# A hybrid decoder layer on one core: cache pages read with four keys per partition, each V tile by one indirect transfer

## The chip, the core and the metric

The kernel runs on one core of a Trainium2 chip. The metric is the device time of one launch in microseconds (us); a run is the median of several executions. Engines are named as in the profile: PE (TensorE, matrix products), DVE (VectorE), ACT (ScalarE), POOL (GpSimd) and SP (SyncE, which here only issues transfers). DMA engines move data between HBM and the on-chip memory SBUF; products land in PSUM.

## What is computed

One decoder layer over 256 prompt tokens and 64 sample tokens (8 sequences of 8 new tokens, each with 2048 cached keys in 16 pages of 128 keys, found through a page table). The layer is a feed-forward block, a mixer of two head groups, and a second feed-forward block. The part that matters here is the sample side of head group A: an indexer picks 256 keys for each query, and attention runs over these. The kernel does it as dense attention over all 2112 keys with a mask, since a key that is not picked gets a very large negative logit:

```python
def sparse_attend(q, qi, wi, pos_q, ki_all, gather_kv, top, rel_bias):
    ...
    _, idx = lax.top_k(score, top)
    valid = idx <= pos_q[None, :, None]
    k_sel, v_sel = gather_kv(idx)
    qg = q.reshape(b, nq, N_KV_HEADS, GQA_GROUP, HEAD_DIM)
    logits = jnp.einsum('bqkgd,bqskd->bqkgs', qg, k_sel).astype(jnp.float32) * HEAD_DIM ** -0.5
    bias = rel_bias[t5_bucket(jnp.maximum(pos_q[None, :, None] - idx, 0))]
    ...
    p = jax.nn.softmax(logits, axis=-1).astype(v_sel.dtype)
    out = jnp.einsum('bqkgs,bqskd->bqkgd', p, v_sel)
```

A softmax over keys and the sum over keys after it don't depend on the order of the keys, as long as logits, mask, bias and values use one order. A page of the K or V cache is 128 keys by 2 heads by 128 numbers in fp32: 1 KB per key, 128 KB per page, contiguous in HBM.

## The kernel before

The program runs in stages: the first feed-forward block (`run_ffn`, L249), the projections of the indexer and its scores (L545 to L717), the threshold search of the top-k (L741 to L770), the projections of q, k and v, then the **sample attention** (L1062 to L1172) together with prompt attention heads (L829) and the last projections (`proj_xbc`, `conv_out`, `proj_z`, L1176 to L1180), then the state-space heads (`ssd_group`, L903) with the output projection `w_out` (L1230), and the second feed-forward block.

A projection streams its weights in chunks of 512 KB (`raw`, three buffers). ACT rounds a chunk to `hi` (L162), DVE makes the remainder `lo` (L163), and PE does three products per tile (L173 to L175). In the sample attention stage the chunks of `w_in` are issued from ACT's queue (`wq[0] = S`, L1174).

The sample attention takes the 8 sequences in 4 pairs `i`, and the 2048 keys of each in 4 blocks `kb` of 4 pages. The loop at L1155 works on the logits of pair `i` and on the outputs of pair `i - 1` in the same turn:

- `load_k` (L1068): per sequence one tile `kn` (512 KB, two buffers in all) from 4 pages, each its own transfer on SP's queue, whose page number SP reads from the page table (`pages`, L508). PE turns each 128 x 128 piece over (L1077, 8 per tile), ACT and DVE copy the result from PSUM (`kt`, L1079).
- `logits_part` (L1083): one mask product (L1085) and four products of the queries with the keys (L1086) into one PSUM tile, copied to `pr` (L1088). After the last block come the new tokens' own keys (L1094), the bias of near keys (L1097) and the softmax (L1098 to L1102).
- `sample_pT` (L1105): 17 transposes of the probabilities.
- `load_v` (L1121) and `out_part` (L1135): two tiles `vn` of 4 pages (512 KB each, four buffers in all), 16 small products (L1136). Of each pair of tiles the first comes through 4 indirect transfers on POOL's queue (L1131), with row numbers from the table `pti`; the second, and both for the last pair, through 4 page transfers on SP's queue (L1129).

The order of the work on PE, ACT, DVE and POOL is not the order of the text: a scheduler in the framework places the instructions when the program is built, by its own costs. Only SP's order in this stage is that of the text (`manual_schedule`, L1064). So a change of the transfers can move other work, projections above all. On the chip every engine then runs its list strictly in order.

Of the kernel before, what the change touches and what calls it, by code (L numbers as in the profile page):

```python
# [10 lines left out]
F32 = mybir.dt.float32  # L11
# [3 lines left out]
I32 = mybir.dt.int32  # L15
AF = mybir.ActivationFunctionType
ALU = mybir.AluOpType
# [4 lines left out]
P = 128  # L22
# [3 lines left out]
NB = 8  # L26
# [7 lines left out]
PAST, PG = 2048, 128  # L34
NPG = PAST // PG
# [10 lines left out]
SK = PAST + TS  # L46
# [3 lines left out]
C_TS, C_TST, C_OH, C_DT, C_TT, C_PI = 512, 576, 640, 1024, 1040, 1048  # L50
# [38 lines left out]
def tile_kernel(tc, I, O, ffn=True):  # L89
    nc = tc.nc  # L90
    V, S, G, TE, SY = nc.vector, nc.scalar, nc.gpsimd, nc.tensor, nc.sync
# [12 lines left out]
    def nm(s):  # L104
        uid[0] += 1
        return f"{s}_{uid[0]}"
# [4 lines left out]
    def pm():  # L111
        return psM.tile([P, 512], F32, tag="m", name=nm("pm"))

    def pa_():
        return psA.tile([P, 512], F32, tag="a", name=nm("pa"))
# [4 lines left out]
    def block(mms, inputs):  # L120

        for m in inputs:
            tc.add_manual_dep(mms[0].ins, m.ins.name, SYNC, reason="block inputs")
        for a, b in zip(mms, mms[1:]):
            tc.add_manual_dep(b.ins, a.ins.name, NOSYNC, reason="block order")
# [3 lines left out]
    def pf():  # L129
        flip[0] += 1  # L130
        return (pw, pm, pa_, pm, pa_, pw, pm, pa_)[(flip[0] - 1) % 8]()

    cst = base.tile([P, C_N], F32, tag="cst", name="cst")
# [10 lines left out]
    def pe_t(out, in_):  # L144
        n = in_.shape[0]
        TE.transpose(out, in_, cst[:n, C_ID:C_ID + n])  # L146
# [181 lines left out]
    per = tc.alloc_tile_pool(name="per", bufs=1)  # L328
# [4 lines left out]
    mkS = per.tile([P, HK], BF, tag="mkS", name="mkS")  # L333
    mkP = per.tile([P, 2, TP], BF, tag="mkP", name="mkP")
    ptb = per.tile([1, NB * NPG], I32, tag="ptb", name="ptb")
    ptc = per.tile([NB * NPG, 1], I32, tag="ptc", name="ptc")
    pti = per.tile([P, NB * NPG], I32, tag="pti", name="pti")
    Rep = per.tile([P, 2, 4, P], BF, tag="Rep", name="Rep")
    saO = per.tile([P, NH, TS], F32, tag="saO", name="saO")
    bS = per.tile([P, 192], F32, tag="bS", name="bS")  # L340
# [88 lines left out]
    pt_flat = I["page_table"].rearrange("b g -> (b g)")  # L429
    SY.dma_start(ptc, pt_flat[:, None])  # L430
    SY.dma_start(ptb, pt_flat[None, :])
    SY.dma_start(pti, pt_flat[None, :].to_broadcast([P, NB * NPG]))
    V.tensor_scalar(pti, pti, float(PG), cst[:, C_PI:C_PI + 1], op0=ALU.mult, op1=ALU.add)
    G.memset(Rep, 0.0)
    for i in range(4):
        sel = cst[:TS, C_ID + 16 * i:C_ID + 16 * i + 16].rearrange("p (b t) -> p b t", b=2)[:, :, None, :].to_broadcast([TS, 2, NH, NS])
# [1 line left out]
            V.tensor_scalar(Rep[TS * half:TS * half + TS, half, i, :].rearrange("p (b h t) -> p b h t", b=2, h=NH), sel, NEG, None, op0=ALU.mult)  # L438

    pre = tc.alloc_tile_pool(name="pre", bufs=1, side="right")  # L440
    csT = per.tile([P, 12, 29], F32, tag="csT", name="csT")
    pc = pm()
    for q in range(3):
# [64 lines left out]
    def pages(pool, b, g0, n):  # L508
        _, vs = nc.values_load_multi_w_load_instructions(ptb[0:1, b * NPG + g0:b * NPG + g0 + n], engines=[SPE], min_val=0, max_val=NPOOL - 1,
                                                         skip_runtime_bounds_check_because="page_table holds page numbers of the pool, as the reference's indexing has it")  # L510
        return [pool[0, ds(v, 1)].rearrange("o p v d -> (o p) (v d)") for v in vs]

    def project(c0, evac):
        ps = [pw(), pw()]
# [45 lines left out]
    for tt in range(3):  # L560
        n = P if tt < 2 else TS
# [19 lines left out]
    def sm(tag):  # L581
        return per.tile([P, 3, SH], F32, tag=tag, name=nm(tag))

    v, e, s_, s2, dt, dA = sm("v"), sm("e"), sm("s_"), sm("s2"), sm("dt"), sm("dA")
# [92 lines left out]
    for u in range(NU):  # L677
# [22 lines left out]
        for par in range(2):  # L700
            src = ps[TS * par:TS * par + TS, :256].rearrange("p (q k g) -> p g k q", q=2, k=8)
# [127 lines left out]
    for h in range(NH):  # L829
        hk = pa.tile([P, 384], F32, tag="hk", name=nm("hk"), bufs=1)  # L830
        src = r_scr[h:h + 1, 0:512]
        SY.dma_start(hk, bass.AP(tensor=src.tensor, offset=src.offset, ap=[[1, P], [1, 384]]))
        kv = h // GQ
        p, pt, po = pm(), pm(), pm()
# [3 lines left out]
        for qt in range(2):  # L838
            nk = P * (qt + 1)
            lg = p[:, lo_[qt]:lo_[qt] + nk]  # L840
# [3 lines left out]
        for qt in range(2):  # L844
            nk = P * (qt + 1)
            lg = p[:, lo_[qt]:lo_[qt] + nk]
# [212 lines left out]
        project(Z0 + j * P, evac)  # L1059


    cv = I["cache_v"][0].rearrange("n k v d -> (n k) (v d)")  # L1062
    order = ExitStack()
    order.enter_context(tc.manual_schedule(engines={SPE}))  # L1064
    def qs(i, q):
        return qS[:, 2 * i + q // 2, 4 * (q % 2):4 * (q % 2) + 4, :].rearrange("p g t -> p (g t)")

    def load_k(i, kb):  # L1068
        kts, made = [], []
        for bb in range(2):  # L1070
            kn = sa.tile([P, 4, 256], F32, tag="kn", name=nm("kn"), bufs=2)
            for g, src in enumerate(pages(I["cache_k"], 2 * i + bb, 4 * kb, 4)):
                SY.dma_start(kn[:, g, :], src)
            for kv in range(2):
                pt = pa_()
                for g in range(4):
                    pe_t(pt[:, g * P:(g + 1) * P], kn[:, g, kv * P:(kv + 1) * P])  # L1077
                kt = sa.tile([P, 512], F32, tag="kt", name=nm("kt"), bufs=5)
                made.append(V.tensor_copy(kt, pt) if kv else S.copy(kt, pt))  # L1079
                kts.append(kt)  # L1080
        return kts, made

    def logits_part(i, kb, pr_, mx, kts, made):  # L1083
        lg = pa_()
        TE.matmul(lg, Rep[:, kb // 2, i, :], mkS[:, 512 * (kb % 2):512 * (kb % 2) + 512], start=True, stop=False)  # L1085
        mms = [TE.matmul(lg[32 * q:32 * q + 32], qs(i, q), kts[q], start=False, stop=True) for q in range(4)]  # L1086
        block(mms, made)
        S.copy(pr_[:, 512 * kb:512 * kb + 512], lg)  # L1088
        if kb < 3:
            V.tensor_reduce(mx[:, kb:kb + 1], pr_[:, 512 * kb:512 * kb + 512], axis=AX.X, op=ALU.max)  # L1090
            return mms
        lg = pa_()
        TE.matmul(lg[:, :TS], Rep[:, 1, i, :], mkS[:, PAST // 2:HK], start=True, stop=False)
        last = [TE.matmul(lg[32 * q:32 * q + 32, :TS], qs(i, q), kT[:, q % 2, TP:T], start=False, stop=True) for q in range(4)]  # L1094
        block(mms[-1:] + last, [])
        S.copy(pr_[:, PAST:SK], lg[:, :TS])
        V.tensor_add(pr_[:, PAST - P:SK], pr_[:, PAST - P:SK], bS)  # L1097
        V.tensor_reduce(mx[:, 3:4], pr_[:, 3 * 512:SK], axis=AX.X, op=ALU.max)  # L1098
        V.tensor_reduce(mx[:, 5:6], mx[:, 0:4], axis=AX.X, op=ALU.max, negate=True)
        S.activation(pr_, pr_, AF.Exp, bias=mx[:, 5:6], accum_out=mx[:, 6:7])  # L1100
        V.reciprocal(mx[:, 6:7], mx[:, 6:7])
        V.tensor_scalar(pr_, pr_, mx[:, 6:7], None, op0=ALU.mult)  # L1102
        return mms + last
# [17 lines left out]
    def load_v(i, kb):  # L1121
        vns, made = [], []
        for bb in range(2):
            vn = sa.tile([P, 4, 256], F32, tag="vn", name=nm("vn"), bufs=4)
            on_sp = pages(I["cache_v"], 2 * i + bb, 4 * kb, 4) if bb or i == 3 else None
            for g in range(4):
                pg_i = (2 * i + bb) * NPG + 4 * kb + g
                if on_sp is not None:
                    made.append(SY.dma_start(vn[:, g, :], on_sp[g]))  # L1129
                else:  # L1130
                    made.append(G.indirect_dma_start(out=vn[:, g, :], out_offset=None, in_=cv, in_offset=bass.IndirectOffsetOnAxis(ap=pti[:, pg_i:pg_i + 1], axis=0)))  # L1131
            vns.append(vn)
        return vns, made

# [20 lines left out]
    for i in range(5):  # L1155
        if i < 4:
            pr_ = sa.tile([P, SK], F32, tag="pr", name=nm("pr"), bufs=1)
            mx = sa.tile([P, 8], F32, tag="mx", name=nm("mx"))
        if i > 0:
            po = pm()  # L1160
        for kb in range(4):
            mms = None
            if i < 4:
                kts, made = load_k(i, kb)
            if i > 0:
                vns, vmade = load_v(i - 1, kb)
            if i < 4:
                mms = logits_part(i, kb, pr_, mx, kts, made)
            if i > 0:
                out_part(i - 1, kb, pT, po, vns, vmade, mms)  # L1170
        if i < 4:
            pT = sample_pT(pr_)  # L1172
# [117 lines left out]
    for tt in range(3):  # L1290
        n = P if tt < 2 else TS
        r = rn[:n, tt:tt + 1]
        p = pf()
        for j in range(4):
            pe_t(p[:n, j * P:(j + 1) * P], xT2[:, 12 + j, tt * P:tt * P + n])
        o = yo[tt][:n]
# [37 lines left out]
```

## Time and profile before

| | |
|---|---|
| median of 3 runs | 2594.49 us (2593.16 to 2596.51) |
| the profiled execution: its own time | 2592.26 us |
| the profiled execution: span in the trace | 2590.2 us |
| PE busy | 2534.6 us (98% of the span) |
| DVE, ACT, POOL busy | 1332.2, 1044.0, 176.9 us |
| mean granted TensorE clock | 0.994 |
| traffic with HBM | 386.00 MB read, 10.88 MB written |

[...] Products are pipelined, so the duration of one is longer than the distance to the next. Queue q1 is SP's, q10 ACT's, q0 POOL's.

### The profile page before, as it was taken

What the parts mean: (1) busy time and instruction counts of PE and PEld (TensorE: products, weight loads), DVE (VectorE), ACT (ScalarE), POOL (GpSimd) and SP (SyncE); (2) the same over time, 40 slices, a digit from 0 to 9 for tenths busy, and PEclk for the clock granted to TensorE, in tenths of its full rate; (3) what the DMA queues carried; (4) which work ended last, traced back from release to release, by engine and by line L of the source; (5) the groups of instructions that cost most, each with busy time, mean ns of one, the idle gap of its engine ahead of it and who ended that gap; (6) DMA issues with size and microseconds to landing.
All of it is one profiled execution on the core that took longest, in us unless ns stands there. A gap on an engine that the chain in (4) does not pass through costs nothing.

```text
span 2590.2 us, 43131 instructions
## 1 busy us (share of the span) xinstructions
PE 2534.6 (98%) x17617; PEld 2442.9 (94%) x17617; DVE 1332.2 (51%) x2052; ACT 1044.0 (40%) x1448; POOL 176.9 (7%) x243
## 2 busy tenths in 40 slices
PE   8999999999999999999999999999999999999997
PEld 6999999999999999788878879999999999999997
DVE  5444444444444456687655566644444444444444
ACT  5333233333333343675644444433333333333333
POOL 3000000000000020001242221100000000000001
PEclk9999999999999999999999999999999999999999
DMA  7444444444445464244787644444444444444443
GB/s 207 139 147 152 150 148 153 147 152 150 146 147 155 143 189 134 81 117 144 221 249 240 187 146 135 138 147 153 148 150 152 148 154 147 150 142 157 153 134 120
DMA packets 401281, 399.70 MB, mean 154 GB/s; under 512 B 22344, under 2 KB 395949, under 8 KB 400572
## 3 DMA queue, kind: packets, MB, share of 16 engines
q1 hardware_dynamic: 366380, 358.76, 44.5%
q10 hardware_dynamic: 30800, 26.23, 3.4%
q0 software_dynamic: 3904, 11.96, 1.5%
q8 instruction: 138, 2.26, 0.4%
q14 instruction: 59, 0.48, 0.1%
HBM read 386.00 MB, written 10.88 MB: 153 GB/s over the span
## 4 chain that ended last, share of the span: by engine, by line
PE 88%; DVE 4%; DMA 2%; ACT 1%; issue 1%; SPq 1%; POOL 0%; ACTq 0%; DVEq 0%; POOLq 0%
PE pw L173 10%; PE pw L174 9%; PE pw L175 9%; PE pa L173 9%; PE pa L174 9%; PE pm L173 9%; PE pa L175 9%; PE pm L175 9%; PE pm L174 9%; DVE lo L163 1%; PE pa L146 1%; PE pm L146 1%; PE pa L687 1%; DMA kn<-in_cache_k_dram 1%; DMA raw<-in_w_in_dram 1%
## 5 line engine op out<-in xcount | busy, mean ns | idle before, releaser
L163 DVE TENSOR_TENSOR lo<-raw,hi 128x1024 fp32r<-128x1024 f32 (+1 forms) x659 | 798.2, 1214 | 868.9 <-ACT hi L162 862.0
L162 ACT CAST hi<-raw 128x1024 fp32r<-128x1024 f32 (+1 forms) x659 | 675.9, 1026 | 1066.9 <-PE pm L174 439.5
L173 PE MATMUL pw<-xh,hi 128*128 128x320 f32 x1360 | 427.6, 314 | 4.2 <-ACT hi L162 1.6
L175 PE MATMUL pw<-xh,lo 128*128 128x320 f32 x1360 | 424.9, 313 | 2.3 <-DVE lo L163 2.3
L174 PE MATMUL pw<-xl,hi 128*128 128x320 f32 x1360 | 425.1, 313 | 1.0 <-DVE xl L198 1.0
L173 PE MATMUL pa<-xh,hi 128*128 128x320 f32 x1056 | 326.5, 309 | 0.3 <-ACT hi L162 0.3
L175 PE MATMUL pa<-xh,lo 128*128 128x320 f32 x1056 | 326.3, 309 | 0.0
L175 PE MATMUL pm<-xh,lo 128*128 128x320 f32 x1056 | 326.2, 309 | 0.0
L174 PE MATMUL pa<-xl,hi 128*128 128x320 f32 x1056 | 326.1, 309 | 0.0
L173 PE MATMUL pm<-xh,hi 128*128 128x320 f32 x1056 | 326.0, 309 | 0.0
L174 PE MATMUL pm<-xl,hi 128*128 128x320 f32 x1056 | 325.7, 308 | 0.0
L173 PEld LDWEIGHTS pw<-xh,hi 128*128 128x128 f32 x1360 | 256.9, 189 | 10.4 <-issue 7.1
L174 PEld LDWEIGHTS pw<-xl,hi 128*128 128x128 f32 x1360 | 256.7, 189 | 5.4 <-issue 3.0
L175 PEld LDWEIGHTS pw<-xh,lo 128*128 128x128 f32 x1360 | 256.9, 189 | 4.7 <-DVE lo L163 2.5
L173 PEld LDWEIGHTS pa<-xh,hi 128*128 128x128 f32 x1056 | 198.5, 188 | 0.7 <-ACT hi L162 0.4
L175 PEld LDWEIGHTS pa<-xh,lo 128*128 128x128 f32 x1056 | 198.6, 188 | 0.2
L175 PEld LDWEIGHTS pm<-xh,lo 128*128 128x128 f32 x1056 | 198.5, 188 | 0.3
L174 PEld LDWEIGHTS pa<-xl,hi 128*128 128x128 f32 x1056 | 198.6, 188 | 0.1
L173 PEld LDWEIGHTS pm<-xh,hi 128*128 128x128 f32 x1056 | 198.6, 188 | 0.1
L174 PEld LDWEIGHTS pm<-xl,hi 128*128 128x128 f32 x1056 | 198.4, 188 | 0.0
L207 POOL TENSOR_TENSOR acc<-acc,sq 128x320 f32<-128x320 f32 x55 | 60.2, 1095 | 1866.5 <-ACT sq L205 1865.6
L173 PE MATMUL pm<-hh,hi 128*128 128x320 f32 x528 | 162.9, 308 | 0.0
(445 smaller groups left out, 3961.5 us busy)
## 6 DMA issues: line engine op xcount, KB each, us to landing
raw<-in_w_ffn_dram SPq DMA_DIRECT2D x511, 512.0 KB
raw<-in_w_in_dram SPq DMA_DIRECT2D x40, 512.0 KB
raw<-in_w_in_dram ACTq DMA_DIRECT2D x40, 512.0 KB
kn<-in_cache_k_dram SPq DMA_DIRECT2D x128, 128.0 KB
raw<-in_w_out_dram SPq DMA_DIRECT2D x32, 512.0 KB
vn<-in_cache_v_dram SPq DMA_DIRECT2D x80, 128.0 KB
raw<-in_w_ffn_dram SPq DMA_DIRECT2D x34, 256.0 KB
hn<-in_state_ssm_dram SPq DMA_DIRECT2D x16, 256.0 KB
```

What stands on the lines that cost most here:

```text
L146: TE.transpose(out, in_, cst[:n, C_ID:C_ID + n])
L162: S.copy(hi, raw)
L163: V.tensor_sub(lo, raw, hi.bitcast(F32))
L173: TE.matmul(out, wh, xh, start=start, stop=False)
L174: TE.matmul(out, wh, xl, start=False, stop=False)
L175: TE.matmul(out, wl, xh, start=False, stop=stop)
L207: (V if k == KT - 1 else G).tensor_add(accs[0], accs[0], sq)
L687: TE.matmul(pr[:, bh * 256:(bh + 1) * 256], qq[:, b].rearrange("p h t -> p (h t)"), kk[:, :, :, b * NPG:(b + 1) * NPG], start=st, stop=not st)
```

## The change

K pages are now read with four neighbouring keys in one partition: page `g` of a tile fills the 32 partitions 32g to 32g+31, with 4 KB in each, where before it filled all 128 partitions with 1 KB in each. So a column of the turned tile is no longer the key of that number, and the keys stand in another, fixed order. The mask product reads its columns in that order, and so does the bias of the near keys, which are now a strided piece of `pr`. A V tile of four pages comes through one indirect transfer on POOL's queue for both sequences and all pairs: 128 rows of 4 KB, with row numbers from a new table `pt4`. SP issues no V transfer any more.

```diff
+    pm4 = pre.tile([P, 1], F32, tag="pm4", name="pm4")
+    for j in range(4):
+        o = slice(32 * j, 32 * j + 32)
+        V.tensor_scalar(pm4[o], cst[o, C_PI:C_PI + 1], -32.0 * j, None, op0=ALU.add)
+        V.tensor_scalar(pt4[o], pti[o].rearrange("p (c j) -> p c j", j=4)[:, :, j], float(PG // 4), pm4[o], op0=ALU.mult, op1=ALU.add)
...
-        return [pool[0, ds(v, 1)].rearrange("o p v d -> (o p) (v d)") for v in vs]
+        return [pool[0, ds(v, 1)].rearrange("o (m r) v d -> (o m) (r v d)", r=4) for v in vs]
...
-    cv = I["cache_v"][0].rearrange("n k v d -> (n k) (v d)")
+    cv = I["cache_v"][0].rearrange("n (m r) v d -> (n m) (r v d)", r=4)
...
-                SY.dma_start(kn[:, g, :], src)
+                SY.dma_start(kn[32 * g:32 * g + 32].rearrange("p r f -> p (r f)"), src)
...
-        TE.matmul(lg, Rep[:, kb // 2, i, :], mkS[:, 512 * (kb % 2):512 * (kb % 2) + 512], start=True, stop=False)
+        TE.matmul(lg, Rep[:, kb // 2, i, :], mkS[:, 512 * (kb % 2):512 * (kb % 2) + 512].rearrange("p (q r) -> p r q", r=4), start=True, stop=False)
...
-        V.tensor_add(pr_[:, PAST - P:SK], pr_[:, PAST - P:SK], bS)
+        near = pr_[:, PAST - 512:PAST].rearrange("p (r q) -> p r q", r=4)[:, :, 96:P]
+        V.tensor_add(near, near, bS[:, 0:P].rearrange("p (m r) -> p r m", r=4))
+        V.tensor_add(pr_[:, PAST:SK], pr_[:, PAST:SK], bS[:, P:192])
...
-            on_sp = pages(I["cache_v"], 2 * i + bb, 4 * kb, 4) if bb or i == 3 else None
-            for g in range(4):
-                pg_i = (2 * i + bb) * NPG + 4 * kb + g
-                if on_sp is not None:
-                    made.append(SY.dma_start(vn[:, g, :], on_sp[g]))
-                else:
-                    made.append(G.indirect_dma_start(out=vn[:, g, :], out_offset=None, in_=cv, in_offset=bass.IndirectOffsetOnAxis(ap=pti[:, pg_i:pg_i + 1], axis=0)))
+            c = (2 * i + bb) * (NPG // 4) + kb
+            made.append(G.indirect_dma_start(out=vn.rearrange("p r f -> p (r f)"), out_offset=None, in_=cv, in_offset=bass.IndirectOffsetOnAxis(ap=pt4[:, c:c + 1], axis=0)))
```

The change also moves the rest of the stage. Up to the sample attention the order of the built program is as before. From there on the scheduler places the projections (`pw` tiles) elsewhere. On PE, at the start of the last pair (the transposes of its first two K tiles, `kn_12940` and `kn_12968`), the order before was this (`Rep`, L1085: the mask product):

```order
L146 MATMUL pa_12954<-cst,kn_12940 128x128 x4
L146 MATMUL pa_12961<-cst,kn_12940 128x128 x4
L146 MATMUL pa_12982<-cst,kn_12968 128x128 x4
L173 MATMUL pw_14506<-xh_8345,hi_14510 128x320
L174 MATMUL pw_14506<-xl_8347,hi_14510 128x320
L175 MATMUL pw_14506<-xh_8345,lo_14511 128x320
L173 MATMUL pw_14506<-xh_8345,hi_14510 128x320
L146 MATMUL pa_12989<-cst,kn_12968 128x128 x4
L1085 LDWEIGHTS Rep
L1085 MATMUL pa_13015<-mkS,Rep 128x512
L174 MATMUL pw_14506<-xl_8347,hi_14510 128x320
L175 MATMUL pw_14506<-xh_8345,lo_14511 128x320
```

From `kn_12940` to the state-space heads some 380 projection products stood between the pieces of the sample attention, the four groups of `proj_z` that begin at `pw_14506`. The same place in the changed program, from the last transposes of the probabilities of the pair before it (`pr_12439`) on, is this (`kn_12832` and `kn_12860` are the first two K tiles of the last pair, L1092 the products of queries and keys):

```order
L146 MATMUL pa_12814<-cst,pr_12439 128x128 x4
L146 MATMUL pa_12820<-cst,pr_12439 128x128 x4
L146 MATMUL pa_12826<-cst,pr_12439 64x128
L146 MATMUL pa_12846<-cst,kn_12832 128x128 x4
L146 MATMUL pa_12853<-cst,kn_12832 128x128 x4
L146 MATMUL pa_12874<-cst,kn_12860 128x128 x4
L146 MATMUL pa_12881<-cst,kn_12860 128x128 x4
L1091 LDWEIGHTS Rep
L1091 MATMUL pa_12892<-mkS,Rep 128x512
L1092 MATMUL pa_12892<-kt_12851,qS 32x512
L1092 MATMUL pa_12892<-kt_12858,qS 32x512
```

No projection product of `w_in` stands behind `kn_12722`, the last K tile of the pair before: all of them have moved ahead, among the pieces of the first three pairs, in runs of 12 and more. Behind it come the whole last pair, the outputs of the last two pairs and only then the products of `w_out`.

On POOL the first V tiles (`vn`) stood like this before, between pieces of the causal convolution (`cn`, `xb`):

```order
L877 COPY cn<-xb_13696 128x24
L1131 DMA vn_12098<-in_cache_v_dram,pti 128x256 x4
L877 COPY cn<-xb_13710 128x3
L873 MEMSET xb_13846 128x3
L874 COPY xb_13846<-csT 128x8x3
```

And now:

```order
L883 COPY cn<-xb_13433 128x24
L1134 DMA vn_12108<-in_cache_v_dram,pt_100 128x1024
L1134 DMA vn_12110<-in_cache_v_dram,pt_100 128x1024
L1134 DMA vn_12192<-in_cache_v_dram,pt_100 128x1024
L1134 DMA vn_12194<-in_cache_v_dram,pt_100 128x1024
L882 COPY cn<-xb_13447 128x3
```

All four V buffers are filled at once at the start, and each later pair of V transfers waits for the products that read the buffers last. POOL issues 32 V transfers where it issued 48, and SP 128 page transfers where it issued 208.

## Rows read from the trace of the kernel before

**Rows 1.** The page, part 1: busy time and share of the span.
```profile
PE 2534.6 (98%) x17617; PEld 2442.9 (94%) x17617; DVE 1332.2 (51%) x2052; ACT 1044.0 (40%) x1448; POOL 176.9 (7%) x243
```

**Rows 2.** Busy time by stretch; last columns granted clock, DMA share, GB/s.
```profile
core 0: us, PE busy (x) PEld busy (x) DVE busy (x) ACT busy (x) POOL busy (x), PEclk, DMA share, GB/s
1200.00:1210.00 10.00, 7.71 (x52) 7.06 (x52) 9.87 (x17) 2.25 (x5) 0.00 (x0) 0.99 0.29 78
1210.00:1220.00 10.00, 8.06 (x33) 6.66 (x31) 5.36 (x15) 5.53 (x11) 4.42 (x8) 0.50 0.66 191
1220.00:1280.00 60.00, 59.97 (x455) 50.32 (x454) 39.31 (x81) 44.68 (x77) 6.72 (x21) 1.00 0.66 196
1280.00:1430.00 150.00, 139.19 (x1369) 117.49 (x1368) 74.41 (x117) 65.98 (x108) 49.40 (x70) 0.98 0.80 243
...
1340.00:1350.00 10.00, 7.19 (x33) 6.57 (x32) 2.40 (x3) 2.10 (x4) 4.61 (x8) 0.66 0.91 292
...
1450.00:1650.00 200.00, 191.54 (x1280) 167.20 (x1279) 135.52 (x212) 96.44 (x185) 49.70 (x47) 1.00 0.43 132
1700.00:1750.00 50.00, 50.00 (x343) 50.00 (x342) 22.19 (x25) 17.20 (x20) 0.00 (x0) 1.00 0.49 153
```

**Rows 3.** Chain that ended last, 1280 to 1430 us: start, us, what.
```profile
1283.07 7.59 DMA raw<-in_w_in_dram
...
1303.99 1.01 PE pm L1136 x32
...
1337.84 5.84 DMA kn<-in_cache_k_dram
...
1353.10 0.99 PE pa L1086 x8
...
1373.55 0.87 PE pa L146 x8
...
1406.70 1.96 PE pa L146 x17
...
1415.83 3.62 DMA vn<-in_cache_v_dram
```

**Rows 4.** SP's queue in order of time, 1318 to 1345 us.
```profile
1324.78 4.99 SPq L1073 DMA_DIRECT2D kn<-in_cache_k_dram  x8
1330.31 6.41 SPq L1129 DMA_DIRECT2D vn<-in_cache_v_dram  x4
1337.31 5.25 SPq L1073 DMA_DIRECT2D kn<-in_cache_k_dram  x8
```

**Rows 5.** DMA queues from 1210 to 1430 us: packets, MB, share of 16 engines; landing.
```profile
q1 hardware_dynamic: 30542, 28.13, 41.9%
...
q0 software_dynamic: 2560, 6.46, 9.7%
...
vn<-in_cache_v_dram,pti POOLq DMA_INDIRECT x48, 4.4
```

**Rows 6.** DMA queue of POOL from 2 to 11 us (the load of x_sample).
```profile
q0 software_dynamic: 284, 0.55, 30.6%
```

**Rows 7.** The second pair's softmax in order of time, 1302 to 1312 us.
```profile
1302.62 0.29 PE L1094 MATMUL pa<-kT,qS 128*32 128x64 f32 x8
...
1304.36 0.74 DVE L1098 TENSOR_REDUCE mx<-pr 128x1 f32<-128x576 f32 x1
...
1306.06 1.28 ACT L1100 ACT_TABLE_LOAD   x1
...
1307.36 2.06 ACT L1100 ACTIVATE pr<-pr,mx 128x2112 f32<-128x2112 f32 x1
...
1309.74 1.32 DVE L1102 TENSOR_SCALAR pr<-pr,mx 128x2112 f32<-128x2112 f32 x1
...
1311.12 1.09 PE L146 MATMUL pa<-cst,pr 128*128 128x128 f32 x8
```

**Rows 8.** Groups by line, 1210 to 1452 us: busy us, mean ns of one.
```profile
L1079 DVE COPY kt<-pa 128x512 f32<-128x512 f32 x32 | 22.0, 687 | 34.5 <-PE pa L146 34.3
L1085 PE MATMUL pa<-mkS,Rep 128*128 128x512 bf16 x16 | 6.3, 393 | 0.0
```

More of the change, by code (lines that the diff above doesn't have):

```diff
@@ L336, in tile_kernel @@
     ptc = per.tile([NB * NPG, 1], I32, tag="ptc", name="ptc")
-    pti = per.tile([P, NB * NPG], I32, tag="pti", name="pti")
+    pt4 = per.tile([P, NB * NPG // 4], I32, tag="pt4", name="pt4")
     Rep = per.tile([P, 2, 4, P], BF, tag="Rep", name="Rep")
@@ L431, in tile_kernel @@
     SY.dma_start(ptb, pt_flat[None, :])
-    SY.dma_start(pti, pt_flat[None, :].to_broadcast([P, NB * NPG]))
-    V.tensor_scalar(pti, pti, float(PG), cst[:, C_PI:C_PI + 1], op0=ALU.mult, op1=ALU.add)
     G.memset(Rep, 0.0)
@@ L440, in tile_kernel @@
     pre = tc.alloc_tile_pool(name="pre", bufs=1, side="right")
+    pti = pre.tile([P, NB * NPG], I32, tag="pti", name="pti")
+    SY.dma_start(pti, pt_flat[None, :].to_broadcast([P, NB * NPG]))
+    pm4 = pre.tile([P, 1], F32, tag="pm4", name="pm4")
[3 more added lines that the diff above has]
+        V.tensor_scalar(pt4[o], pti[o].rearrange("p (c j) -> p c j", j=4)[:, :, j], float(PG // 4), pm4[o], op0=ALU.mult, op1=ALU.add)
     csT = per.tile([P, 12, 29], F32, tag="csT", name="csT")
```

## Prediction

> **What bounds the kernel now.** Read the page's busy line first: PE is busy 98% of the span [rows 1], so time can only come from stretches in which PE waits, and be lost where it waits anew. Next come the stretches by time. In the feed-forward block PE never waits: 343 products in 50.00 us, 0.146 us each [rows 2]. Up to the sample attention the built program keeps its order, and so its times. The attention stage begins near 1210 us. Its first part has no gap (59.97 of 60 us busy); from 1280 to 1430 us PE is busy 139.19 of 150 us: 10.8 us of waiting [rows 2]. The chain that ended last names what it waited for: nine pieces of DMA, for K pages, V pages and weight chunks, the longest 7.59 us [rows 3]. That is a stretch of crowded transfers: the DMA engines are busy 0.80 of it. SP's list shows the crowding too: four V transfers took 6.41 us to issue, while eight K transfers took 4.99 us, and the K transfers behind them stood still [rows 4]. One gap also cost clock: from 1340 to 1350 us the granted clock was 0.66, after PE had stood, so some 7.19 x 0.34 = 2.4 us of slower work [rows 2]. After 1450 us another 8.5 us of waiting lie in 200 us [rows 2]. **At most about 13 us stand to be won in this stage.**
>
> **What the change does, part by part.**
>
> *The tables* (eight small DVE instructions for `pt4` in place of one for `pti`) run during the first feed-forward block, where DVE is idle half of the time: nothing. *The mask product* reads its moving operand in a strided order, 16 times; at 0.39 us each [rows 8] even a doubling adds 6 us of PE work. I take nothing, since the same bytes are read; 0 to 6 is the bound. *The bias* becomes two adds of the same elements, four times: a fraction of a microsecond each, inside the softmax waits below.
>
> *Larger packets.* This is the visible aim, so price it: SP's queue, with 1 KB packets, moved 28.13 MB in 41.9% of 16 engines' 220 us, 52.4 us of one engine per MB. POOL's queue, with the V rows, needed 9.7% for 6.46 MB, 52.9 us per MB [rows 5]. Its packets were already 2560 for 6.46 MB, so larger. **The size of a packet buys no engine time** by these rows.
>
> *K into 32 partitions.* No row shows this. One transfer before went to fewer partitions: x_sample into 64. It held 30.6% of 16 engines for 9 us, 0.55 MB: 80 us per MB [rows 6], one and a half times the usual price. The bound is 52.4 below (no loss), and above 105, twice that, if half as many partitions again take half the rate. I take 80, the nearest row. [...]
>
> *V off SP's queue.* SP loses 80 of 208 page transfers; in its list a page takes about 0.6 us (4.99 us for eight), so K pages come earlier. POOL issues 32 transfers in place of 48. It has little else to do here (49.40 of 150 us) [rows 2], and an indirect transfer landed 4.4 us after issue [rows 5]. With all four buffers filled early, V is a whole turn ahead. So the waits for K, V and weights go: gain 10.8 + 2.4 = **13 us**.
>
> *The order.* Here is the loss. The projections were what PE did while a softmax ran or a page travelled. Some 380 of them, 380 x 0.146 = 56 us, stood between the start of the last pair and the state-space heads; now none does. They run earlier, where PE is then busy throughout, with pages far ahead. Their work is the same; what is lost is the cover. Count PE's idle time from the last projection on:
> - The rest of the third pair's last block: PE waits for the copies of the last K tile (0.69 us [rows 8]) and for the hand-over of the outputs: 2 us.
> - Softmax of the third pair: in the second pair it took from 1302.9, the end of the last logits, to 1311.1, the first transpose: 8.2 us [rows 7]. Two of these are covered by output products (1.01 us a block [rows 3]). Idle 6 us. Then the clock: after PE had idled 2.3 of ten us, and more at the start of the next ten, 0.50 was granted [rows 2]. So 17 transposes of 1.96 us [rows 3] take twice that: 2 us.
> - Four blocks of the last pair. PE has two tiles of transposes (2 x 0.87), 0.39 of mask, 0.99 of logits and 1.01 of outputs [rows 3, 8], 4.1 us, and waits 0.7 for copies. With two K buffers, a tile is called for only when the tile before last is turned. A block needs at least SP's eight issues, 5 us [rows 4], and at most, by DMA time, 1.05 MB of K at 80 and as much V at 52.9 over 16 engines, 5.2 + 3.5 = 8.7 us. The first block is there already (1 us idle); for three I take 8 us, near the upper end since K and V arrive together: 1 + 3 x 4 = 13 us idle.
> - The last pair's softmax and transposes, as above: 8 us.
> - The last V tiles: their buffers come free only when the first two blocks of the last outputs are done. Issue and landing are some 1 + 4.4 us, less 1 us of other work: 4.5 us.
> - The hand-over of the outputs to the `w_out` products, through ACT and DVE: 2.5 us.
>
> Together 2 + 8 + 13 + 8 + 4.5 + 2.5 = **38 us** lost. Behind it, state and `w_out` loads are now issued while nothing else runs: I give back 2 of the 8.5 us. Sum: 38 - 13 - 2 = 23 us. The profiled execution took 2592.3 us, so 2615 us; it stands 2.2 us under the median of the runs, so **2617 us**.
>
> **The rivals.**
>
> [...] K at 105 us per MB makes a block 6.9 + 3.5 = 10.4 us, 7 us more in three blocks. Gaps of 4 us between pieces may hold the clock at 0.50, as after the idle time near 1210 us [rows 2]; the tail has some 30 us of PE work, of which half might run at half speed beyond what is counted, 8 us more. Sum 2617 + 7 + 8 = 2632 us. For it: the row of x_sample, the 0.66 and 0.50 stretches. [...]
>
> *Faster.* The place is the same tail. If a block is paced by SP's issues alone (5 us: 1 us idle each, 4 us for four), if each softmax is 2.5 us shorter because ACT and DVE have no convolution pieces and no activation table between its steps (1.28 us for the table alone [rows 7]), and if the clock stays, then 1 + 3.5 + 4 + 3.5 + 1.5 + 1.5 = 15 us are lost. Against them stand 13 us, and up to the 8.5 us after 1450 us, if those waits are for the state and weight loads that now come early: 2592.3 + 15 - 21.5 + 2.2 = 2588 us. It decides at 16 us of loss in the tail. Against it: both softmax waits have no work behind them in the new order, and nothing removes them.
>
> *No change.* The same with 16 to 26 us lost in the tail: some 2594 us.
>
> That K is still cut into 1 KB pieces, so that the change doesn't do what it says, would alter nothing: the price per MB is the same [rows 5], and the order has moved anyway.
>
> **How the numbers follow.** A difference under about 0.2%, 5 us, can't be told from none here. The forecast gets 0.58, the worse tail 0.22, the faster case 0.10, no change 0.10. The first two are slower: 0.80. The forecast's own bounds are 5 to 8.7 us a block (minus 9, plus 2) and the mask product (plus 6), so 2608 to 2625. For 8 in 10 the range runs from the no-change case at 2596 to beyond the worse tail, 2638.
>
> **What would show it.** Right: between 1280 us and the last projection PE has next to no gap; then some 65 us with PE idle for more than half, in two stretches of 6 us or more with only DVE and ACT at work, and waits for `kn` at each block; the granted clock falls in them; the state-space heads start some 20 us later than before. The share of the queues shows K's price per MB: over 52.4 or not. Wrong: waits for raw chunks or V in the part with projections; a tail under 50 us; no waits at `kn` there; or a gain behind 1500 us of more than 3 us.

## The result and the profile after

The changed kernel takes **2619.86 us** (median of 4 runs, 2615.99 to 2622.71); the kernel before, on the same chip, 2595.26 us. The ratio is 1.0095, 95% interval 1.0082 to 1.0107: slower by 24.6 us. The forecast was 2617 us. The profiled execution took 2621.16 us (span 2619.4), 28.9 us more than that of before.

PE is busy for 2544.9 us of the span where it was for 2534.6 [rows 1], and idle for 74.5 where it was for 55.6. Where this comes from, the table of stretches shows; its columns are those of [rows 2], the granted clock as a share of TensorE's full clock. The first line is the part with projections, the second the whole tail, from the last projection to the state-space heads, and then the tail by pieces: rest of the third pair's last block, its softmax, its transposes, the four blocks of the last pair, its softmax, its transposes, the last outputs. The last line is the start of the state-space heads.

```profile
1280.00:1399.90 119.90, 119.47 (x1039) 108.69 (x1039) 65.73 (x97) 54.42 (x79) 15.94 (x28) 1.00 0.78 212
1399.90:1473.10 73.20, 45.96 (x497) 32.67 (x495) 21.26 (x34) 21.98 (x38) 16.61 (x20) 0.75 0.69 201
1399.90:1404.80 4.90, 4.22 (x68) 2.42 (x66) 2.46 (x5) 1.91 (x5) 0.76 (x1) 1.00 0.81 193
1404.80:1410.20 5.40, 0.10 (x2) 0.03 (x1) 1.64 (x3) 3.64 (x5) 1.11 (x2) 0.90 1.05 354
1410.20:1413.80 3.60, 3.60 (x17) 3.54 (x18) 0.69 (x1) 1.17 (x2) 0.00 (x0) 0.50 0.09 34
1413.80:1451.10 37.30, 25.22 (x248) 16.66 (x246) 13.41 (x20) 10.41 (x18) 6.68 (x7) 0.74 0.78 216
1451.10:1454.90 3.80, 0.16 (x2) 0.06 (x1) 1.48 (x2) 2.28 (x4) 1.16 (x2) 0.81 0.93 282
1454.90:1458.70 3.80, 3.80 (x21) 3.42 (x23) 0.84 (x2) 1.17 (x2) 0.00 (x0) 0.50 0.25 99
1458.70:1473.10 14.40, 8.85 (x150) 6.54 (x149) 0.74 (x2) 1.40 (x3) 6.89 (x10) 0.74 0.48 153
1473.10:1503.00 29.90, 23.95 (x132) 18.39 (x129) 14.54 (x17) 11.23 (x31) 11.82 (x11) 0.87 0.45 143
```

Where 10.8 of 150 us were waited before [rows 2], 0.43 of 119.9 us are now: that gain is real. In the tail PE stands for 73.20 - 45.96 = 27.2 us, and the clock of 0.75 costs another 46.0 x 0.25 = 11.5 us: 38.7 us. (The clock's part is an estimate: it takes every product in a slow stretch for longer by the missing clock.) The last line shows a loss that the forecast did not have: 5.95 us idle and 24.0 x 0.13 = 3.1 us of clock, 9.1 us; the same 30 us of the kernel before had 2.07 us idle at full clock:

```profile
1452.00:1482.00 30.00, 27.93 (x190) 21.92 (x189) 19.83 (x25) 16.60 (x38) 10.57 (x10) 1.00 0.40 118
```

What PE waited for in the last pair (waits, 1413.8 to 1473.1 us; total, times, longest):

```profile
PE pa L146 <- DMA kn<-in_cache_k_dram: 8.8, 4, 3.4
PE pa L146 <- DVE pr L1110: 3.6, 1, 3.6
...
PE pm L1139 <- DMA vn<-in_cache_v_dram,pt: 2.7, 2, 1.4
```

The chain there answers to [rows 3] and [rows 7]. Read it for what stands in it: a softmax with nothing of PE between its steps, transposes of 3.86 us where they were 1.96, a K page, and the last V tiles, issued by POOL only when their buffers come free. The longest piece is a chunk of `w_out` (11.27 us), whose rounding on ACT and remainder on DVE stand ahead of the last softmax's work on these engines; by the trace they held it up by some 0.6 us only.

```profile
1405.06 1.28 ACT L1108
1406.35 2.15 ACT pr L1108 x2
...
1408.73 1.33 DVE pr L1110
...
1423.43 6.69 DMA kn<-in_cache_k_dram
...
1435.92 11.27 DMA raw<-in_w_out_dram
...
1454.87 3.86 PE pa L146 x17
1458.73 1.85 PE pm L1139 x32
...
1464.50 5.98 DMA vn<-in_cache_v_dram,pt
```

SP's queue there, for [rows 4]: the pages of three blocks, 6.7 us a block, waits for free buffers among them, after SP had waited for the first buffer since 1404 us.

```profile
1415.79 20.03 SPq L1079 DMA_DIRECT2D kn<-in_cache_k_dram  x24
```

For [rows 5], the queues from 1210 to 1400 us (packets, MB, share of 16 engines):

```profile
q10 hardware_dynamic: 15840, 15.73, 30.9%
q1 hardware_dynamic: 5255, 13.58, 28.5%
q0 software_dynamic: 2580, 9.41, 15.4%
```

K, on q1, costs 0.285 x 16 x 190 / 13.58 = 64 us of one engine per MB, where 52.4 were usual; V, on q0, costs 50. And for [rows 8], the mask product (groups by line):

```profile
L1091 PE MATMUL pa<-mkS,Rep 128*128 128x512 bf16 x16 | 9.8, 615 | 0.0
```

It went from 393 to 615 ns by its strided reading: 16 x 0.22 = 3.5 us. (e5 and e6, in one order on PE, show it too: 610 ns strided, 389 ns in the old order.)

At the start of the state-space heads PE waited 2.8 us for `xd`, the first write of the heads (e12 is about this), and as long again for a DVE cast, `selE`:

```profile
PE pm L955 <- DVE selE L950: 2.9, 1, 2.9
PE pm L146 <- DVE xd L918: 2.8, 1, 2.8
```

The cast took 0.41 us in the kernel before, beside the last projections, and 3.87 us now, while POOL was at work:

```profile
1427.71 0.41 DVE L945 CAST selE<-sel 48x512 fp32r<-48x512 f32 x1
```
```profile
1483.36 3.87 DVE L950 CAST selE<-sel 48x512 fp32r<-48x512 f32 x1
```

The loads of the state come later than before, not earlier: SP issues them behind other loads, and had stood before those for 17.3 us for the last V tiles. Before, then now:

```profile
1431.51 6.78 SPq L967 DMA_DIRECT2D hn<-in_state_ssm_dram  x4
```
```profile
1476.12 4.73 SPq L972 DMA_DIRECT2D hn<-in_state_ssm_dram  x4
```

### The profile page after: what moved, and what is told of

The parts are those of the page before. It is cut to its first block, busy times and chain, and to the rows that moved or that the text cites. A ratio compares the mean times of both kernels' runs of the same rounds, so it can differ in the third digit from the quotient of the medians.

```text
span 2619.4 us, 42877 instructions
## 1 busy us (share of the span) xinstructions
PE 2544.9 (97%) x17617; PEld 2455.1 (94%) x17617; DVE 1333.3 (51%) x2063; ACT 1042.3 (40%) x1446; POOL 160.4 (6%) x227
## 4 chain that ended last, share of the span: by engine, by line
PE 88%; DVE 5%; DMA 2%; ACT 2%; issue 1%; SPq 0%; POOL 0%; ACTq 0%; DVEq 0%
PE pw L174 10%; PE pw L173 10%; PE pw L175 10%; PE pa L174 9%; PE pa L173 9%; PE pa L175 9%; PE pm L173 9%; PE pm L174 9%; PE pm L175 9%; DVE lo L163 1%; PE pa L146 1%; PE pm L146 1%; PE pa L692 1%; PE pm L703 1%; DMA raw<-in_w_ffn_dram 0%
```

## The experiments

The theory (A): the loss is the missing cover, whatever the transfers are. The rival (B): the new transfers cost the time by themselves. All ratios are to the kernel before on the same chip, with a 95% interval. The kernel before itself came out at 2588.71 us in the set of e1 to e4 and at 2593.28 us in that of e5 to e8, on one chip, so a comparison across sets is uncertain by some 5 us.

**e1: the old transfers with the new order.**

```diff
     for i in range(5):
+        if i == 3:
+            wq[0] = S
...
+            for j in (0, 2, 4, 6):
+                proj_z(j)
+            wq[0] = SY
```

> The kernel before with its own transfers (K in 128 partitions, V by pages), but the calls of the ten projections are written ahead of the last pair, so that all of them stand before it on PE, as in the changed kernel. Theory A (the order is the loss: the last pair has nothing to cover its waits): slower than before by 25 to 45 us, 2620 to 2640 us, since the waits before the last pair stay partly and the exposed blocks are paced by 8 K and 8 V page transfers of SP. Theory B (the new transfers are the loss, K in 32 partitions and V on POOL's queue alone): no more than 8 us from before, 2587 to 2603 us.

Measured 2614.23 us against 2588.71: 1.0098 (1.0080 to 1.0115), 25.5 us. A holds: with the transfers of before, taking the cover from the last pair costs as much as the whole change. Its bare stretch (columns as above) is 21.5 us idle at a clock of 0.84. What ends the waits is another transfer, V on SP's queue (10.6 us), with K hardly waited for (1.6 us).

```profile
1421.00:1475.30 54.30, 32.78 (x407) 22.80 (x406) 14.73 (x23) 13.54 (x24) 8.71 (x9) 0.84 0.68 204
```
```profile
PE pm L1136 <- DMA vn<-in_cache_v_dram: 10.6, 4, 4.6
...
PE pa L146 <- DMA kn<-in_cache_k_dram: 1.6, 3, 0.9
```

**e2: K alone.**

```diff
-                SY.dma_start(kn[:, g, :], src)
+                SY.dma_start(kn[32 * g:32 * g + 32].rearrange("p r f -> p (r f)"), src)
...
+                kp = kt.rearrange("p (g m r) -> p r g m", g=4, r=4)
+                pp = pt.rearrange("p (r g m) -> p r g m", r=4, g=4)
```

> Only the K pages are read as in the change (four keys per partition, 32 partitions a page); the copies of the turned K tiles out of PSUM put the keys back into their old order, so mask product, bias and V transfers are those of before. The program is laid out anew and again all projections stand ahead of the last pair; by its order 6 of the 16 blocks have no projection beside them where the changed kernel has 4. Theory A (order): slower than the changed kernel too, 2620 to 2645 us, as its exposed blocks also wait for V pages on SP. Theory B1 (V on POOL alone is the loss): within 5 us of before, 2590 to 2600 us.

2623.87 us against 2588.71: 1.0143 (1.0124 to 1.0161). K alone makes the scheduler move all projections ahead, and V on POOL's queue is not needed for the loss: B1 falls. (The longer copies, 1.05 to 1.08 us against 0.59 and 0.69, are in it.)

**e3 and e4: an order by hand, with the new and the old transfers.** A generator hands out the projections in pieces, and ordering dependencies on PE chain them with the pieces of the sample attention:

```diff
+    FILL = [(1, 1, 4), (1, 3, 2), (1, 3, 2), (1, 3, 2), (0, 3, 0)]
...
+                fill(FILL[i][0])
                 mms = logits_part(i, kb, pr_, mx, kts, made)
...
+            fill(FILL[i][1])
         if i < 4:
+            fill(FILL[i][2])
             pT = sample_pT(pr_)
```

> All transfers, mask, bias and V of the changed kernel; only the order on PE is written by hand: the ten projections are cut into 80 pieces of 12 products (1.75 us) and spread over the whole sample attention, one between the turning of a K block and its logits, three behind each block's outputs, five in each softmax. Theory A (order): the tail's loss goes and the gain of the faster transfers stays, 13 us or more under before, 2570 to 2583 us. Theory B (transfers): the waits for K stay, spread over the stage; no faster than before, 2593 to 2615 us.

> The kernel before with its own transfers and the same order by hand as the run before. Theory A: nearly as fast as the new transfers in this order, slower by the waits that SP's queue makes where K and V pages share it, 2575 to 2592 us. Theory B (the new transfers cost time by themselves): faster than the new transfers in the same order by 8 us or more.

New 2635.33 us (1.0182, 1.0165 to 1.0199), old 2614.62 (1.0102, 1.0084 to 1.0120). Neither reaches the times of theory A, and e3 is slower than B had it too; only B's condition, old transfers faster than new ones by 8 us or more, is met. The order was a bad one: with the projections chained to the attention, the prompt heads ahead of it had no cover. From 1180 to 1300 us e3 has PE idle for 29.5 of 120 us at a clock of 0.84 (before: 7.2 us, 0.96). But the new transfers came out 20.7 us behind the old ones, which A does not explain; as the two differ around the heads too, a cleaner pair was needed.

**e5, e6 and e7: the same with the heads covered**, three transfers in one order. e7 replaces the K pages:

```diff
-            for g, src in enumerate(pages(I["cache_k"], 2 * i + bb, 4 * kb, 4)):
-                SY.dma_start(kn[32 * g:32 * g + 32].rearrange("p r f -> p (r f)"), src)
+            c = (2 * i + bb) * (NPG // 4) + kb
+            G.indirect_dma_start(out=kn.rearrange("p r f -> p (r f)"), out_offset=None, in_=ck, in_offset=bass.IndirectOffsetOnAxis(ap=pt4[:, c:c + 1], axis=0))
```

> The changed kernel's transfers once more with an order by hand, as in the run e3, which had taken the projections away from the prompt heads at its start. Here three of the ten projections stay free for the scheduler to place among the prompt heads, and only the last seven, 56 pieces of 12 products, are spread: one piece between the turning of a K block and its logits, two (in the last pair one) behind each block's outputs, two to four more in each softmax. Theory A (the loss is the missing cover, the transfers are good): nothing is exposed for long, 5 to 15 us under before. Theory B (the new transfers cost time by themselves, as e3 against e4 hints with 20.7 us): slower than before, and slower than the old transfers in the same order by 8 us or more.

> The kernel before with its own transfers and the order of the run e5; on PE the two differ by a few rows in the first pair only. Theory A: within 5 us of the new transfers in this order, or slower. Theory B: faster than these by 8 us or more.

> As e5, but each K tile too comes by one indirect transfer on POOL's queue, as the V tiles do: 128 rows of 4 KB into 128 partitions, the keys where the change puts them. SP issues no page at all. If K's 62 us per MB of the changed kernel (before: 52.4) come from the 32 partitions of a page, the price falls to V's 50 us per MB; if they come from the traffic, it stays near 60. Time: 0 to 12 us under e5 where K is what is waited for; if POOL's queue holds K up behind V transfers that wait for their buffers, slower than e5 by 5 us or more.

| | median us | ratio to before |
|---|---|---|
| e5, new transfers | 2619.75 | 1.0098 (1.0073 to 1.0124) |
| e6, old transfers | 2601.56 | 1.0030 (1.0018 to 1.0043) |
| e7, K and V indirect, 128 partitions | 2595.14 | 1.0010 (1.0000 to 1.0019) |

So A is only half of it. With cover everywhere the new transfers still lose 18.2 us to the old ones, as B had it, and reading the same rows into 128 partitions wins 24.6 us back, twice the most that was expected of e7. K's price falls, too. K and V of e7 are both on q0, from 1250 to 1440 us: 0.452 x 16 x 190 / 28.76 = 47.8 us per MB.

```profile
q0 software_dynamic: 8105, 28.76, 45.2%
```

e7 changed two things, the partitions and the queue. e9 and e10 change the partitions alone.

**e8: three K buffers, three V buffers** (`bufs=2` to 3 at `kn`, 4 to 3 at `vn`).

> The changed kernel with three K buffers in place of two and three V buffers in place of four; the last pair stands as bare on PE as in the changed kernel. If the number of K buffers paces the exposed blocks (the theory of the prediction), the waits for K there, 10.6 us together in the changed kernel, fall by 4 us or more in the first two blocks, and the run is 3 to 8 us faster than the changed kernel. If the transfers' own time paces them, or the fewer V buffers take it back, the same within 3 us, or slower.

2622.87 us, 1.0115 (1.0092 to 1.0137): no gain. The waits for K in the bare pair fell from 8.8 to 5.7 us, those for V rose from 2.7 to 11.0: the third K buffer was paid for with a V buffer, and the run can't tell what a third K buffer alone would be worth. It shows that the pace of a bare block isn't set by K's buffers alone.

```profile
PE pm L1139 <- DMA vn<-in_cache_v_dram,pt: 11.0, 6, 2.7
PE pa L146 <- DMA kn<-in_cache_k_dram: 5.7, 2, 4.3
```

**e9 and e10: the K page in 32 partitions that lie four apart**, in the changed kernel's order and in that of e5.

```diff
-                SY.dma_start(kn[32 * g:32 * g + 32].rearrange("p r f -> p (r f)"), src)
+                SY.dma_start(kn.rearrange("(m g) r f -> g m (r f)", g=4)[g], src)
...
+                kp = kt.rearrange("p (r g m) -> p r g m", r=4, g=4)
+                pp = pt.rearrange("p (r m g) -> p r g m", r=4, g=4)
```

> The changed kernel, its order on PE the same row by row; only the 32 partitions of a K page are others: page g goes to partitions g, g + 4, g + 8 and so on, over all 128, in place of 32 neighbours. Queue, packets of 4 KB and number of transfers stay. The copies of the turned K tiles put the keys back in the order of the changed kernel, which makes each longer, by about 0.45 us (1.05 to 1.08 us in the run e2 against 0.59 and 0.69). If the 32 neighbouring partitions are what makes K dear, its price falls from 62 to about 50 us per MB, the waits for K in the bare last pair fall by 4 us or more, and the run is 3 to 10 us faster than the changed kernel. If SP's queue or the traffic makes it dear, the price stays within 3 of 62 and the run is the same or up to 6 us slower.

> The same edit in the order by hand of the run e5 (2619.75 us): on PE it differs from e5 by nothing. If the neighbouring partitions are the cause of the 18 us that the new transfers cost in that order against the old ones, 8 us or more of them go, to 2600 to 2612 us; if not, 2615 to 2625 us.

This is the run that settles K's price. Queues from 1250 to 1440 us in e5, 32 neighbours:

```profile
q1 hardware_dynamic: 5854, 15.61, 32.7%
q10 hardware_dynamic: 12649, 12.56, 24.8%
q0 software_dynamic: 3136, 10.65, 17.4%
```

and in e10, 32 partitions over all 128:

```profile
q1 hardware_dynamic: 5864, 15.80, 26.2%
q10 hardware_dynamic: 12144, 12.06, 21.0%
q0 software_dynamic: 3706, 12.73, 19.6%
```

On q1 the price falls from 63.7 to 50.4 us per MB, and what travels beside K gets cheaper as well: the weights (q10) from 60.0 to 52.9, V (q0) from 49.7 to 46.8. The waits of PE for K, in e5 (1250 to 1470 us) and in e10 (1250 to 1450 us):

```profile
PE pa L146 <- DMA kn<-in_cache_k_dram: 16.8, 8, 7.4
```
```profile
PE pa L146 <- DMA kn<-in_cache_k_dram: 8.7, 5, 4.6
```

e10 takes 2603.45 us (1.0059, 1.0043 to 1.0074), as the first theory had it: it lies 15.4 us over the kernel before on its chip, where e5 lay 26.5 over it on another, so some 11 us (16 by the times themselves) hang on which 32 partitions a page fills. The copies, which the expectation of e9 took to be 0.45 us longer by this edit, were not: 688 and 582 ns on DVE and ACT, against 687 and 583 in the changed kernel. What e10 still loses to e6, 7.5 us by the ratios, was not taken apart; the mask product's 3.5 us are in it. K's price into neighbouring partitions was 63.7 / 50.4 = 1.26 times that into spread ones; why, no run shows.

e9, the same edit in the changed kernel's own order, missed: 2622.99 us (1.0137, 1.0121 to 1.0152), not faster than the changed kernel but if anything slower, though the price fell there too. In its last pair (1412 to 1450 us, with `w_out` chunks on q1) it is 0.392 x 16 x 38 / 4.80 = 49.7 us per MB, against 0.479 x 16 x 38 / 4.72 = 61.7 in the changed kernel (e9 first, then the changed kernel). The waits for K stayed: 8.3 us against 8.8.

```profile
q1 hardware_dynamic: 2809, 4.80, 39.2%
```
```profile
q1 hardware_dynamic: 2736, 4.72, 47.9%
```
```profile
PE pa L146 <- DMA kn<-in_cache_k_dram: 8.3, 3, 3.8
```

So in the changed kernel's order K's price is hidden: while projections run, pages are early at either price (up to the bare pair PE was busy for 185.6 of 192.0 us in e9 and for 185.5 of 191.9 in the changed kernel), and in the bare pair a block waits for the round of buffer, issue and landing, which a cheaper transfer did not shorten. (Longer copies don't hide a gain here either: they took 688 and 585 ns in e9, and PE's waits for them are 1.6 us in both.)

**e11: a version meant to win.** The transfers of e7, heads and first pair left to the scheduler (the diff is against e7):

```diff
-    FILL = [(1, 0, 4), (1, 2, 2), (1, 2, 2), (1, 1, 4), (0, 2, 0)]
+    FILL = [(0, 0, 0), (1, 2, 2), (1, 2, 2), (1, 2, 2), (0, 2, 0)]
...
+            if i == 0:
+                for j in (8, 10, 0, 2, 4, 6)[:3]:
...
+                linked[0] = True
```

> A version meant to beat both kernels: K and V by one indirect transfer a tile, into 128 partitions, as in e7; prompt heads and first pair are left to the scheduler, which places three projections there as in the kernel before (e7 lost most of its time there), and the other seven are spread over the last three pairs by hand, 8 to 10 pieces a pair more than there is need of none. If e7's loss lies in the heads alone, 5 to 12 us under before, 2581 to 2588 us. If POOL's queue or the transfers hold the stage, within 3 us of before.

2590.37 us against 2588.03: 1.0006 (0.9997 to 1.0015), no different from before. By the ratios it lies 23 us under the changed kernel, but its interval overlaps that of e7: what e7 failed to gain did not lie in the heads alone, and no version here beats the kernel before.

**e12: the loss at the state-space heads.** In the changed kernel `xd` (DVE, the first write of the heads) waits for the stores of the convolution's last rows (what `xd` waited for, and POOL's list in order of time): they come behind the last V transfers.

```profile
  DMA out_dram<-cvo: 5.1, 1
```
```profile
1464.50 0.94 POOL L1134 DMA_INDIRECT vn<-in_cache_v_dram,pt  x1 [0.30 <-issue]
1465.44 0.60 POOL L902 DMA_DIRECT2D out_dram<-cvo  x1
...
1475.00 0.51 POOL L902 DMA_DIRECT2D out_dram<-cvo  x1 [2.29 <-ACT cvo L901]
...
1481.88 1.04 POOL L939 TENSOR_TENSOR xdd<-xd,dec 128x512 f32<-128x512 f32 x1 [5.85 <-DVE xd L918]
```

```diff
-            G.dma_start(O[5][0, 0, :, 384 * q:384 * q + 384], co[0:3])
-            G.dma_start(O[10][0].rearrange("b r c -> (b r) c")[:, 384 * q:384 * q + 384], co[3:27])
+            S.dma_start(O[5][0, 0, :, 384 * q:384 * q + 384], co[0:3])
+            S.dma_start(O[10][0].rearrange("b r c -> (b r) c")[:, 384 * q:384 * q + 384], co[3:27])
```

> The changed kernel with one edit: the eight stores of the convolution's last rows (cvo) are issued from ACT's queue in place of POOL's. In the changed kernel they stand on POOL behind the last V transfers, from 1465 us (in the kernel before from 1411 us), and the state-space heads' first write (xd) waits 5.1 us for them. If that explains the 8 us that are lost after the last outputs, beyond the bare attention, 4 to 8 us under the changed kernel, a ratio to before of 1.0063 to 1.008 (the changed kernel: 1.0095). If the state-space heads start late for another reason (the clock, selE on DVE), within 2 us of the changed kernel.

2617.84 us, 1.0114 (1.0097 to 1.0130). In the trace the wait is gone, and the start of the heads loses 3.3 us idle and 3.0 us of clock where it lost 9.1 in the changed kernel:

```profile
1472.00:1503.00 31.00, 27.72 (x190) 22.61 (x189) 14.99 (x19) 12.46 (x32) 10.50 (x9) 0.89 0.50 159
```

What is left there is the other wait: PE still stands 2.6 us for `selE`, whose cast again took 3.91 us beside POOL. The expected 4 to 8 us did not come: the ratio overlaps that of the changed kernel, and if anything is higher. That the stores cause the wait is shown; that they are worth 3 us or more is not.

## Why the prediction was right, and where it was not

The time, the sign and the place were right, the time in part by luck: errors of several us made up for each other. Of the signs that it named, two did not come: PE was idle for 27.2 of the tail's 73.2 us, not for more than half, and the two bare softmaxes were 5.4 and 3.8 us, not 6 or more. By its own terms:

- **Gain 13 us** (waits before the last projection): it went as said; 0.43 us of waiting are left in 119.9 us at a clock of 1.00.
- **Tail 38 us**: 38.7 measured, but by terms that were off and made up for each other. Idle time was 27.2 us where 34 were counted (2 + 6 + 13 + 6 + 4.5 + 2.5 with the clock left out): the rest of the block 0.7 for 2, the softmax 5.3 for 6, the four blocks 12.1 for 13, the last softmax 3.6 for 6, the last V tiles and the hand-over 5.6 for 7. The clock took 11.5 us where 4 were counted. The transposes came out as forecast (0.50 granted, 1.8 us each time), but the four blocks ran at 0.74 as well, 25.2 x 0.26 = 6.6 us, which the prediction had kept for its rival of 2632 us, the "worse tail".
- **Give back 2 us**: this step failed. Only the `w_out` loads come early (from 1403 us on, before from 1438 us); those of the state come at 1476 us, 5 us ahead of `xd`, where they came 22 us ahead of it. And the start of the state-space heads loses 7 us more than before (9.1 against 2.1), not less. The prediction named every transfer that POOL no longer issues, but not what POOL issues behind the last V tiles: the convolution's stores, which moved with the projections from 1411 us to 1465 us and later (2.8 us of PE's waiting). As much again (2.9 us) is the cast `selE`, which before ran early, beside projections, and now met POOL's work. The late state loads were not what PE waited for there.
- **Mask product 0**: 3.5 us, inside its bound of 0 to 6.
- **K at 80 us per MB** (52.4 to 105): 62 to 64. The nearest row, x_sample into 64 partitions, was compared with a price from another stretch. In its own 9 us [rows 6] SP's queue, into 128 partitions, paid 0.691 x 16 x 9 / 1.50 = 66 us per MB, so x_sample cost 1.2 times its neighbours, not one and a half times; 1.2 x 52.4 is 63. In this kernel's order the term hardly mattered: e9 took the price back to 50 and won nothing. Under another order it would have been some 11 us (e10). SP's queue from 2 to 11 us, in the kernel before:

```profile
q1 hardware_dynamic: 1387, 1.50, 69.1%
```

- **The size of a packet buys no engine time**: 4 KB packets over 128 partitions cost 47 to 50 us per MB (V in e10 46.8, K and V in e7 47.8, V in the changed kernel 50), 1 KB packets 52.4: 5 to 10% less, on another queue. The prediction's nothing was nearly right.
- **The sum.** The measured terms, 38.7 + 7 + 3.5 - 13, give 36 us, and the profiled executions differ by 28.9. About 2 us of the gap lie in the first 100 us of the span, where PE was idle for 10.6 us and before for 12.6. The other 5 us are open; that the clock's terms are too high is likely, not shown.

The cause is shown from one side by e1: the order alone, with old transfers, costs 25.5 us. From the other side the prediction would have misled: it speaks of the order as the loss, and an engineer who put the projections back would have found e5, as slow as the change. The two losses don't add up, as each hides the other: the new transfers cost 18.2 us in the spread order (e5 against e6) and nothing that shows in the bare one (24.6 us with them, 25.5 in e1). With the projections all ahead, K's price is covered there and the tail is bare; with the projections spread, the tail is covered and K's price shows. What stays open is the pace of a bare block: neither a third K buffer at the cost of a V buffer (e8) nor a cheaper K (e9) shortened it, and the `w_out` chunks that SP issues between the K pages were not taken out alone.

## What to carry to other kernels

When a scheduler places the work, read first where a change of transfers puts the cover: here a bare last stage cost its waits (27.2 us idle), and then the clock on top of them (0.75, by estimate 11.5 us), with the new transfers as with the old (e1: 21.5 us idle at a clock of 0.84). Before calling that the cause, put the old order under the new transfers as well as the new order under the old ones; either loss alone can be the whole difference (here 25.5 us in e1 and 26.5 in e5, of 24.6). Read also what else moves with the cover: here small stores and a cast did, which cost 7 us at the start of the next stage. Where a load must fill few partitions, try them spread over the whole range, and look at what the other queues pay beside it: in the order of e5 that took K from 63.7 to 50.4 us per MB, the weights beside it from 60.0 to 52.9, and some 11 us off the time; in the changed kernel's own order it won nothing (e9).

## What was not expected of the hardware

- The same 32 packets of 4 KB per page cost 63.7 us of an engine per MB into 32 neighbouring partitions and 50.4 into 32 that lie four apart (e5, e10); weights beside them went from 60.0 to 52.9.
- The mask product (128x512), its moving operand read with a step of four bf16 numbers, took 615 ns instead of 393, and at full clock too: the eleven of the changed kernel up to 1390 us took 610 to 612 ns each, where most of the kernel before took 376 to 379.
- The cast `selE` on DVE (48x512) took 0.41 us in 23 of its 28 places in the fourteen traces, and 2.9 to 3.9 us in the other five (the changed kernel, e1, e8, e9, e12). These five alone began while a POOL product ran, and each ended 0.3 us after the last of two or three such products in a row, in the changed kernel at 1487.23 us, POOL's at 1486.95. In e2, where POOL's product began 0.16 us after the cast, the cast took 0.41 us. No run took POOL's work away by itself.
- A copy of 128x512 fp32 out of PSUM took as long as a plain one (687 and 583 ns in the changed kernel) when it read with a step of four numbers (688 and 585 ns in e9), but 1.07 and 1.08 us when it wrote to SBUF with such a step (e2).
- SP's issues of K pages stood still, by the profile's reading of the waits, for weight chunks that ACT had issued: 20.6 us in e5 and 6.2 us in e10, in e5 once for 8 us between the first and the second page of one tile. Why SP waited for them, no run shows. Waits of SP's queue in e5 (1250 to 1470 us) and e10 (1250 to 1450 us):

```profile
SPq L1106 <- DMA raw<-in_w_in_dram: 20.6, 6, 7.9
```
```profile
SPq L1106 <- DMA raw<-in_w_in_dram: 6.2, 4, 3.6
```
